# Storing the residual gate in rows of 512 bytes, and loading a gate tile behind its unit's weights

## The chip, the cores and the metric

The kernel runs on one core of one Trainium2 chip. The metric is the device time of one execution in microseconds (us), the median of several runs. Lower is better.

## The reference: one layer of a hybrid diffusion block

256 latent tokens and 256 context tokens of width 2048 pass through one layer: a modulated norm, one wide input projection, a bidirectional recurrent branch of 16 heads (RWKV-7), a latent attention branch of 8 heads, and a merge. Only the end matters for the change:

```python
sh_x, sc_x, g_x = modulation(c, w_mod[i], b_mod[i])      # g_x: the residual gate, 2048 values
...
def merge_branches(o_rwkv, o_mla, gate_logits, w_br_r, w_br_m, w_out):
    g_r, g_m = jnp.split(jax.nn.sigmoid(gate_logits), 2, axis=-1)
    return (g_r * (o_rwkv @ w_br_r) + g_m * (o_mla @ w_br_m)) @ w_out
...
x_new = x + g_x * merge_branches(o_rw_x, o_ml_x, mg_x, w_branch_rwkv[i], w_branch_mla[i], w_out[i])
```

So there are two kinds of gates: the *merge gates* (`gate_logits`, 2 x 2048 values for each token) and the *residual gate* `g_x` (one value for each of the 2048 columns).

## The kernel before: how the work is staged

**Matmuls.** Every large matmul is done in three passes for accuracy. A weight piece `w` of 128 x 512 float32 is loaded by SP's DMA queue (L236, in `piece`), ScalarE (ACT) casts it to a high part `wh`, VectorE (DVE) subtracts to get a low part `wl` (both in `parts_of`, through helpers whose line is L141), and TensorE (PE) runs high x high, high x low and low x high (L114, L116, L119). A *half* of a unit is one weight piece: four blocks of 128 by 128, thus 12 matmuls. `weights` issues the loads of both pieces of a unit first, and then hands them out one by one:

```python
247  def weights(src, n, pool=None, ns=None):
249      ws = [piece(src[:, n // 2 * i:n // 2 * i + n // 2], [P, n // 2], pool) for i in range(2)]
250      for w in ws:
251          yield parts_of(w, pool, ns)
```

**Buffers.** Up to a switch late in the kernel, the pool `wp` holds 4 buffers for `w`, 3 for `wh`, 2 for `wl`. After the switch (`place[:] = mg, NWL, NSX, NSX`, L1437) units use the pool `mg`, with 8, 4 and 4. The gate tiles `th` have 2 buffers in `wp` and 4 in `mg`.

**Order.** A scheduler sets one static order for each engine, from priorities and from a planner's estimate; the casts and subtractions of weights (`HP`) get priority. At run time each engine, and SP with its DMA issues too, goes through its own list strictly in order. An instruction whose semaphores are not there holds up everything behind it on the same engine.

**Stages.** The norm and the first projection come first. The recurrent branch follows, with further projections running between its steps as background work (the units of `bg_z`, `merge_gate_g` and others). Then comes attention, whose background ends with the first merge branch. The second merge branch (`w_br[1]`) and the output projection (`w_out`) end the kernel.

**The residual gate.** 32 small products with `w_mod_g` run as background in the recurrent stage and are summed into `gT`, 128 partitions x 16 columns: the value of gate column 128 c + p stands at partition p, column c. It goes to a DRAM tile `gd` of 16 x 128 (L1450), and is read back four times for the output projection, each time as four rows repeated for all partitions (`gx`, L1472). The store of L1450 writes through a transposed view, so each run in memory is one float32 of 4 bytes. In the program it stands behind the attention, but it waits for nothing but `gT`, and the scheduler puts it into the recurrent stage.

**The merge's first branch.** `merge_gate_g` has left tanh of each merge gate in the DRAM tile `thd`. `branch_g(j)`, j = 0 to 15, is one unit of background work: it loads the gate tile `th` (L1400), multiplies two halves of `w_br[0, j]`, forms (th + 1) x product on DVE, in place in `th`, and stores it back to `thd` (L1409), from where the second branch reads it (`gth`, L1456):

```python
1397 def branch_g(j):
1399     th = logits()
1400     nc.sync.dma_start(th, thd[j])
1401     ps = pp.tile([P, 512], F32, name="acc", tag="acc", bufs=2)
1402     for i, (wh, wl) in enumerate(weights(w_br[0, j], 1024)):
...
1408     V.scalar_tensor_tensor(th, th, 1.0, ps[:, 0:T], ALU.add, ALU.mult)
1409     nc.sync.dma_start(thd[j], th)
```

Units 0 to 11 take their `th` from `wp`, so a load there waits until the store two units earlier has landed and left its buffer. Units 12 to 15 take it from `mg`. The product goes to one of two `acc` buffers, so the matmuls of unit j + 2 wait for DVE's step of unit j. In the order listings below a unit is known by its numbers: before, `th_14902` with `acc_14904` is unit 7, `th_14953` unit 8, `th_15117` unit 12, and the weights are `w_14997`, `w_14999` (unit 9), `w_15038`, `w_15040` (10), `w_15079`, `w_15081` (11), `w_15120`, `w_15122` (12) and `w_15161`, `w_15163` (13). In the changed kernel the weights' numbers are lower by 2, and `th` is numbered after its weights (`th_14911` is unit 7, `th_14962` unit 8, `th_15126` unit 12).

Of the kernel before, what the change touches and what calls it, by code (L numbers as in the profile page):

```python
# [9 lines left out]
F32 = mybir.dt.float32  # L10
# [6 lines left out]
P = 128  # L17
D = 2048
KT = D // P
# [126 lines left out]
def hybrid_block(  # L146
# [20 lines left out]
    nc = tc.nc  # L167
    clock = Clock()
    V, S = Elementwise(nc.vector, clock, 960, 0.066), Elementwise(nc.scalar, clock, 1200, 0.08)
    E = Tensor(nc.tensor, clock)  # L170
# [12 lines left out]
    def con(name):  # L183
        o, w = CO[name]
        return cc[:, o:o + w]
# [5 lines left out]
    ident = con("ident")  # L191
# [41 lines left out]
    def piece(src, shape, pool=None):  # L233

        w = (pool or place[0]).tile(shape, F32, name="w", tag="w", bufs=NWU if pool else place[1])
        nc.sync.dma_start(w, src)  # L236
        return w

    def parts_of(w, pool=None, ns=None):

        h = (pool or place[0]).tile(list(w.shape), F32R, name="wh", tag="wh", bufs=ns or place[2])
        l = (pool or place[0]).tile(list(w.shape), F32R, name="wl", tag="wl", bufs=ns or place[3])
        with tc.high_priority(HP):
            split(w, h, l)
        return h, l

    def weights(src, n, pool=None, ns=None):

        ws = [piece(src[:, n // 2 * i:n // 2 * i + n // 2], [P, n // 2], pool) for i in range(2)]
        for w in ws:  # L250
            yield parts_of(w, pool, ns)

    def mm3(ps, ah, al, bh, bl, start, stop):

        E.matmul(ps, lhsT=ah, rhs=bh, start=start, stop=False)
        E.matmul(ps, lhsT=ah, rhs=bl, start=False, stop=False)
        E.matmul(ps, lhsT=al, rhs=bh, start=False, stop=stop)
# [16 lines left out]
    pp = ctx.enter_context(tc.tile_pool(name="pp", bufs=2, space=PSUM))  # L274
# [157 lines left out]
    gT = cst.tile([P, KT], F32, name="gT")  # L432
# [33 lines left out]
    thd = dr1.tile([2 * KT, P, T], F32, name="thd")  # L466
# [688 lines left out]
    with tc.tile_pool(name="ml", bufs=2) as ml:  # L1155
# [238 lines left out]
        def logits():  # L1394
            return wp.tile([P, T], F32, name="th", tag="th", bufs=2)

        def branch_g(j):

            th = logits()
            nc.sync.dma_start(th, thd[j])  # L1400
            ps = pp.tile([P, 512], F32, name="acc", tag="acc", bufs=2)
            for i, (wh, wl) in enumerate(weights(w_br[0, j], 1024)):
                with E.burst(tc):
                    for k in range(4):
                        cs = slice(128 * k, 128 * k + 128)
                        mm3(ps[:, 0:T], wh[:, cs], wl[:, cs], *(t[:, 4 * i + k] for t in ob[0]), i + k == 0, i * 4 + k == 7)
                yield
            V.scalar_tensor_tensor(th, th, 1.0, ps[:, 0:T], ALU.add, ALU.mult)
            nc.sync.dma_start(thd[j], th)  # L1409

        brought = False
        for j in range(KT):
            main.append(((lambda j=j: brought and len(extra) == 0), branch_g(j)))
# [15 lines left out]
    mg = ctx.enter_context(tc.tile_pool(name="mg", bufs=2))  # L1429
# [14 lines left out]
    while gate_left:  # L1444
        ps = pp.tile([P, 512], F32, name="acc", tag="acc", bufs=2)
# [1 line left out]
    if gsum:  # L1447
        gate_sum()
    gd = dr1.tile([KT, P], F32, name="gd")
    nc.sync.dma_start(gd.rearrange("c p -> p c"), gT)  # L1450
    mh = mg.tile([P, KT, T], F32R, name="mh", bufs=1)
    ml_ = mg.tile([P, KT, T], F32R, name="mlo", bufs=1)
    for j in range(KT):
        th = [mg.tile([P, T], F32, name=f"gth{b}") for b in range(2)]
        for b in range(2):
            nc.sync.dma_start(th[b], thd[16 * b + j])  # L1456
        ps = pp.tile([P, 512], F32, name="chp", tag="ch", bufs=2)
# [149 lines left out]
```

## Time and profile before

| What | Value |
|---|---|
| time, median of 3 runs | 1277.62 us (1274.62 to 1279.53) |
| the profiled execution: its own time, and its span | 1277.28 us, 1275.5 us |
| PE busy | 1211.3 us, 95% of the span |
| DVE busy, ACT busy | 953.0 us (75%), 577.1 us (45%) |
| DMA | 212.10 MB, mean 166 GB/s; 68560 of 172320 packets under 512 B |
| mean granted PE clock | 0.992 |

PE = TensorE, PEld = its weight loads, DVE = VectorE, ACT = ScalarE, SPq = SyncE's DMA issues. Times within the profile count from the start of the span. In a row of the timeline, the figure in brackets is how long the engine stood idle before the instruction, and what ended that. A stretch of the windows view gives busy us for each engine, then the granted clock (1.00 is full speed), the share of time in which the DMA engines were busy, and GB/s.

### The profile page before, as it was taken

The page shows a single profiled execution, that of the slowest core. Times are in us where ns is not written, and L with a number is a line of the kernel's source. Part 1 is how long each engine was busy: PE and PEld are TensorE (multiplying, and loading weights), DVE is VectorE, ACT ScalarE, POOL GpSimd, SP SyncE. Part 2 cuts the span into 40 slices and gives each one's busy share as a digit, 9 for nine tenths or more (in the row PEclk, how much of TensorE's full clock was granted, in tenths as well). Part 3 has the DMA queues.
Part 4 walks back from the last instruction along what each step waited for, and adds up shares of the span by engine and source line. Part 5 has one row for each costly group of instructions (what it writes and reads, how often), then busy time and mean ns, then how long its engine had stood idle before and what let it go on. Part 6 is the DMA issues. An engine that isn't in the chain of part 4 may idle for free. (4 is left out here: it accounts for less than half of the span.)

```text
span 1275.5 us, 30066 instructions
## 1 busy us (share of the span) xinstructions
PE 1211.3 (95%) x11484; PEld 1027.0 (81%) x11484; DVE 953.0 (75%) x2658; ACT 577.1 (45%) x1215; POOL 3.3 (0%) x9
## 2 busy tenths in 40 slices
PE   5999999999999989999999997999999999899998
PEld 2566878778887877887788787989899999899887
DVE  4444777877898878888978886875876777769655
ACT  3444543442444424524434343444565555535443
POOL 0000000000000000000000000000000000000000
PEclk9999999998999999999999998999999999999999
DMA  9998445443442434533434354434765433589684
GB/s 375 355 365 313 134 143 166 145 127 103 132 121 84 137 80 112 141 111 102 140 92 146 83 148 118 114 81 148 229 212 167 123 118 109 182 274 295 225 259 140
DMA packets 172320, 212.10 MB, mean 166 GB/s; under 512 B 68560, under 2 KB 96848, under 8 KB 171664
## 3 DMA queue, kind: packets, MB, share of 16 engines
q1 hardware_dynamic: 172176, 210.18, 52.9%
q8 instruction: 90, 1.47, 0.5%
q14 instruction: 54, 0.44, 0.1%
HBM read 195.30 MB, written 14.82 MB: 165 GB/s over the span
## 5 line engine op out<-in xcount | busy, mean ns | idle before, releaser
L141 ACT CAST wh<-w 128x512 fp32r<-128x512 f32 (+1 forms) x484 | 290.9, 607 | 359.4 <-PE acc L119 139.4
L141 DVE TENSOR_TENSOR wl<-w,wh 128x512 fp32r<-128x512 f32 (+1 forms) x480 | 322.4, 674 | 145.2 <-ACT wh L141 70.6
L119 PE MATMUL acc<-hmh,wl 128*128 128x256 f32 (+1 forms) x1312 | 398.3, 304 | 5.3 <-DVE wl L141 4.9
L119 PE MATMUL acc<-hml,wh 128*128 128x256 f32 (+1 forms) x1312 | 394.9, 301 | 0.0
L119 PE MATMUL acc<-hmh,wh 128*128 128x256 f32 (+1 forms) x928 | 274.2, 296 | 0.0
L119 PEld LDWEIGHTS acc<-hmh,wl 128*128 128x128 f32 x1312 | 249.2, 190 | 20.7 <-DVE wl L141 9.2
L119 PEld LDWEIGHTS acc<-hml,wh 128*128 128x128 f32 x1312 | 250.0, 191 | 9.3 <-issue 1.0
L119 PEld LDWEIGHTS acc<-hmh,wh 128*128 128x128 f32 x928 | 176.8, 190 | 4.9
L116 PE MATMUL acc<-hmh,wh 128*128 128x256 f32 (+1 forms) x384 | 145.2, 378 | 13.1 <-ACT wh L141 8.6
L116 PEld LDWEIGHTS acc<-hmh,wh 128*128 128x128 f32 x384 | 72.8, 190 | 38.9 <-ACT wh L141 14.8
L141 DVE TENSOR_TENSOR pr<-wt 64x14 f32<-64x14 f32 (+6 forms) x224 | 42.6, 190 | 3.4
L141 DVE TENSOR_TENSOR wt<-wt,pr 64x14 f32<-64x14 f32 (+6 forms) x224 | 42.3, 189 | 3.3
L114 PE MATMUL a<-hmh,wh 128*128 128x512 f32 x96 | 40.7, 424 | 0.0
L141 DVE TENSOR_TENSOR W<-WT,lv 128x512 f32<-128x512 f32 x48 | 32.2, 683 | 8.7 <-PE lv L114 8.7
L114 PE MATMUL pm<-wm,ssil 128*32 128x256 f32 x512 | 34.5, 385 | 4.5 <-DMA wm<-in_w_mod_ss 4.4
L114 PE MATMUL a<-hmh,wl 128*128 128x512 f32 x96 | 38.0, 395 | 0.4 <-DVE wl L141 0.4
L114 PE MATMUL a<-hml,wh 128*128 128x512 f32 x96 | 37.9, 395 | 0.0
L114 PE MATMUL lv<-W,Z 64*64 64x64 f32 x1024 | 33.8, 220 | 3.9 <-DVE W L141 3.9
L114 PEld LDWEIGHTS lv<-W,Z 64*64 64x64 f32 x1024 | 31.7, 135 | 5.9 <-DVE W L141 5.1
L114 PE MATMUL chp<-obh,wh 128*128 128x256 f32 x128 | 36.2, 283 | 0.0
L114 PE MATMUL chp<-obl,wh 128*128 128x256 f32 x128 | 36.2, 283 | 0.0
L114 PE MATMUL chp<-obh,wl 128*128 128x256 f32 x128 | 36.2, 283 | 0.0
(324 smaller groups left out, 2164.6 us busy)
## 6 DMA issues: line engine op xcount, KB each, us to landing
w<-in_w_proj SPq DMA_DIRECT2D x296, 256.0 KB, 3.0
wm<-in_w_mod_ss SPq DMA_DIRECT2D x64, 512.0 KB, 7.3
w<-in_w_mod_g SPq DMA_DIRECT2D x64, 256.0 KB, 3.1
w<-in_w_br SPq DMA_DIRECT2D x64, 256.0 KB, 4.1
w<-in_w_out SPq DMA_DIRECT2D x64, 256.0 KB, 3.5
w<-in_w_first SPq DMA_DIRECT2D x32, 192.0 KB, 4.9
thd<-th SPq DMA_DIRECT2D x48, 128.0 KB, 3.1
xT<-in_xcT SPq DMA_DIRECT2D x4, 1024.0 KB, 9.0
```

The costliest lines, as they stand in the source:

```text
L114: return self.engine.matmul(out, lhsT=lhsT, rhs=rhs, **kw)
L116: self.head.append(self.engine.matmul(out, lhsT=lhsT, rhs=rhs, **kw))
L119: i = self.engine.matmul(out, lhsT=lhsT, rhs=rhs, **kw)
L141: return fn(out, *a, **kw)
```

## The change

Two edits. In `branch_g` the tile `th` is made, and its load issued, inside the loop when the first half arrives: behind both weight loads of the unit instead of ahead of them. And `gT` is transposed on PE into a PSUM tile of 16 x 128, copied by ACT to a new tile `gr`, and stored to `gd` from there, as 16 rows of 512 bytes.

```diff
         def branch_g(j):
-            th = logits()
-            nc.sync.dma_start(th, thd[j])
             ps = pp.tile([P, 512], F32, name="acc", tag="acc", bufs=2)
             for i, (wh, wl) in enumerate(weights(w_br[0, j], 1024)):
+                if not i:
+                    th = logits()
+                    nc.sync.dma_start(th, thd[j])
                 with E.burst(tc):
...
     gd = dr1.tile([KT, P], F32, name="gd")
-    nc.sync.dma_start(gd.rearrange("c p -> p c"), gT)
+    ps = pp.tile([P, 512], F32, name="wk", tag="wk", bufs=2)
+    E.transpose(ps[0:KT, 0:P], gT, ident)
+    gr = mg.tile([KT, P], F32, name="gr", bufs=1)
+    S.copy(gr, ps[0:KT, 0:P])
+    nc.sync.dma_start(gd, gr)
```

In SP's list, in the recurrent stage: a weight piece, the gate's store, two weight pieces, a store of the recurrent output. First before, then after.

```order
L236 DMA w_10417<-in_w_proj 128x512
L1450 DMA gd_15281<-gT_1344 128x16x1
L236 DMA w_10466<-in_w_proj 128x512
L236 DMA w_10468<-in_w_proj 128x512
L1076 DMA orwd_1354<-y_10087 128x256
```

```order
L236 DMA w_10417<-in_w_proj 128x512
L236 DMA w_10466<-in_w_proj 128x512
L236 DMA w_10468<-in_w_proj 128x512
L1076 DMA orwd_1354<-y_10087 128x256
L236 DMA w_10512<-in_w_proj 128x512
```

The gate's store has left this place, and the weight pieces follow each other. The engines' lists stand otherwise as before up to the first merge branch.

In SP's list in the first merge branch, from the store of unit 6 on, before and then after:

```order
L1409 DMA thd_1348<-th_14840 128x256
L236 DMA w_15038<-in_w_br 128x512
L1400 DMA th_15117<-thd_1348 128x256
L1400 DMA th_14953<-thd_1348 128x256
L236 DMA w_15120<-in_w_br 128x512
L236 DMA w_15040<-in_w_br 128x512
L236 DMA w_15122<-in_w_br 128x512
L236 DMA w_15079<-in_w_br 128x512
```

```order
L1410 DMA thd_1348<-th_14849 128x256
L236 DMA w_15036<-in_w_br 128x512
L236 DMA w_15118<-in_w_br 128x512
L1403 DMA th_14962<-thd_1348 128x256
L236 DMA w_15120<-in_w_br 128x512
L236 DMA w_15038<-in_w_br 128x512
L1403 DMA th_15126<-thd_1348 128x256
L236 DMA w_15077<-in_w_br 128x512
```

Unit 12's first weight piece has moved ahead of unit 8's gate load, and unit 12's gate load behind both of its pieces. Unit 12's second piece still follows unit 8's gate load. Units 0 to 11 had their gate loads behind their own weights already: the scheduler had put those loads, which wait for a buffer, there.

DVE's list at the same place (`obl` is the low part of attention's output), before and then after:

```order
L141 TENSOR_TENSOR wl_15018<-w_14999,wh_15017 128x512
L141 TENSOR_TENSOR wl_15125<-w_15120,wh_15124 128x512
L141 SCALAR_TENSOR_TENSOR th_14902<-th_14902,acc_14904 128x256
L141 TENSOR_TENSOR wl_15141<-w_15122,wh_15140 128x512
L141 SCALAR_TENSOR_TENSOR th_14953<-th_14953,acc_14955 128x256
L141 TENSOR_TENSOR wl_15043<-w_15038,wh_15042 128x512
L141 TENSOR_TENSOR wl_15166<-w_15161,wh_15165 128x512
```

```order
L141 TENSOR_TENSOR wl_15018<-w_14997,wh_15017 128x512
L141 TENSOR_TENSOR wl_15123<-w_15118,wh_15122 128x512
L141 TENSOR_TENSOR wl_15141<-w_15120,wh_15140 128x512
L141 SCALAR_TENSOR_TENSOR th_14911<-th_14911,acc_14902 128x256
L141 SCALAR_TENSOR_TENSOR th_14962<-th_14962,acc_14953 128x256
L141 TENSOR_TENSOR wl_15164<-w_15159,wh_15163 128x512
L141 TENSOR_TENSOR wl_15182<-w_15161,wh_15181 128x512
```

DVE's step of unit 7 now stands behind both of unit 12's subtractions instead of one, and that of unit 8 follows it at once.

The store of the gate is now here, in SP's list between the store of unit 10 and the loads of the second branch:

```order
L1410 DMA thd_1348<-th_15003 128x256
L1403 DMA th_15249<-thd_1348 128x256
L1410 DMA thd_1348<-th_15044 128x256
L1455 DMA gd_15281<-gr_15284 16x128
L1461 DMA gth0_15289<-thd_1348 128x256
L1403 DMA th_15085<-thd_1348 128x256
```

It waits for ACT's copy `gr`. PE's transpose stands between units 8 and 9, and ACT's copy right behind the cast of unit 12's second piece.

## Prediction

> **What bounds the kernel.** The page comes first: PE is busy for 95% of the span and leads the chain that ended last. What can be won is PE's idle time and its slow time.
>
> ```profile
> PE 1211.3 (95%) x11484; PEld 1027.0 (81%) x11484; DVE 953.0 (75%) x2658; ACT 577.1 (45%) x1215; POOL 3.3 (0%) x9
> PE 33%; DMA 4%; DVE 1%; ACT 1%; issue 0%; SPq 0%; DVEq 0%; ACTq 0%
> ```
>
> DMA's part of that chain is small, so the question is where it sits. The list of DMA issues (count, KB each, median us to landing):
>
> ```profile
> w<-in_w_proj SPq DMA_DIRECT2D x296, 256.0 KB, 3.0
> dl<-AQ SPq DMA_DIRECT2D x128, 8.0 KB, 1.5
> gd<-gT SPq DMA_DIRECT2D x1, 8.0 KB, 12.2
> ```
>
> The gate's store moves 8 KB in 12.2 us. `dl` moves 8 KB in runs of 64 bytes and lands in 1.5 us; the gate's runs have 4 bytes, so there are 2048 of them. Weight pieces (time to landing, min/median/max) from 500 to 700 us and from 765 to 800 us:
>
> ```profile
> DMA to landing us min/median/max: 2.4/3.0/5.5
> ```
>
> ```profile
> DMA to landing us min/median/max: 2.5/3.2/13.2
> ```
>
> One piece beside the gate's store took 13.2 us. SP's timeline, then the chain of waits, name it:
>
> ```profile
> 777.00 0.45 SPq L1450 DMA_DIRECT2D gd<-gT  x1
> 777.67 2.88 SPq L236 DMA_DIRECT2D w<-in_w_proj  x2
> ```
>
> ```profile
> 777.67 13.20 DMA w<-in_w_proj
> ...
> 790.97 0.62 ACT wh L141
> 791.58 0.29 ACT th L141
> ```
>
> The piece issued right behind the gate's store lands at 790.87. ACT's cast `wh` waits for it, and the activation `th` stands behind that cast. PE's timeline and two windows (PE, PEld, DVE, ACT, POOL busy; clock; DMA share; GB/s) show the damage:
>
> ```profile
> 784.85 0.60 PE L126 MATMUL wk<-cc,BK 128*128 128x128 f32 x4
> 791.64 0.58 PE L116 MATMUL acc<-hmh,wh 128*128 128x256 f32 x1 [6.19 <-ACT wh L141]
> 792.98 0.58 PE L119 MATMUL acc<-hmh,wl 128*128 128x256 f32 x1 [0.54 <-DVE wl L141]
> 797.64 0.60 PE L126 MATMUL wk<-cc,BK 128*128 128x128 f32 x4
> 797.99 0.36 PE L116 MATMUL acc<-hmh,wh 128*128 128x256 f32 x1
> ```
>
> ```profile
> 792.00:794.00 2.00, 1.46 (x7) 1.16 (x6) 1.93 (x6) 1.58 (x3) 0.00 (x0) 0.50 0.16 43
> 794.00:796.00 2.00, 2.00 (x11) 2.00 (x11) 1.71 (x8) 0.62 (x1) 0.00 (x0) 0.50 0.67 222
> ```
>
> PE stands idle for 6.19 us, and then runs at a granted clock of 0.50.
>
> **Part 1, the gate's store.** What leaves this place is the 4-byte store. The pieces behind it keep their order, and with the usual 3.0 us the first of them would land at about 780.7, before ACT wants it. The price has three readings.
>
> The lowest is the idle time alone, 6.2 us. The highest counts PE alone. From the transposes at 784.85 to those at 797.64 PE did two halves in 12.79 us. At full clock a half takes 1.40 us, by these two pieces of the chain (each is 11 of a half's 12 matmuls):
>
> ```profile
> 1129.35 1.29 PE acc L119 x11
> 1130.75 1.29 PE acc L119 x11
> ```
>
> Four transposes take 0.35 us (797.64 to 797.99). So 3.15 us would do, and 9.6 us come back.
>
> The third asks what is late next, and that is DVE with ACT. DVE, ACT and PE, in this order:
>
> ```profile
> 791.90 0.42 DVE L141 SCALAR_TENSOR_TENSOR gz<-th,acc 128x256 f32<-128x256 f32 x1 [7.81 <-ACT th L141]
> 797.89 0.69 DVE L141 TENSOR_TENSOR wl<-w,wh 128x512 fp32r<-128x512 f32 x1 [0.81 <-PE acc L119]
> 803.54 1.28 DVE L141 TENSOR_TENSOR_SCAN En<-restart,En 128x260 f32<-128x260 f32 x2
> ```
>
> ```profile
> 799.77 0.66 ACT L141 COPY wt<-wt 64x256 f32<-64x256 f32 x1 [0.67 <-DVE wt L141]
> ```
>
> ```profile
> 806.06 0.39 PE L119 MATMUL acc<-hmh,wl 128*128 128x256 f32 x1 [0.15 <-DVE wl L141]
> ```
>
> DVE's `gz` needs the finished unit, whose matmuls end just ahead of the transposes (about 785.0), and ACT's `th`, some 0.4 us: it can start at about 785.5, not 791.90, so 6.4 us earlier. From there DVE works nearly without a gap; only its wait of 0.81 us for PE at 797.89 drops out, as PE is then further ahead. That makes 7.2 us. ACT's copy `wt` waits for DVE, the activations behind it feed DVE's scan at 803.54, and PE waits at 806.06 for a `wl` that stands behind that scan. So PE's lead beyond DVE's is given back there, all but some 0.1 us. I take **7.3 us**, since PE is seen to wait for DVE there, and keep 6.2 and 9.6 as ends.
>
> What the edit adds: one PE transpose (0.15 us, a quarter of the 0.60 at 797.64) and one small ACT copy (under the 0.62 us of a cast). Both stand in the branch, where PE is about to wait 3.23 us and ACT waits for weights (next part), so they cost nothing; without that cover, under 0.8 us. The new store has 16 runs of 512 bytes. By its bytes and its fewer runs it should land like `dl`, in 1.5 us, at most like a weight piece in 3.0. It is issued some 16 us ahead of its first reader:
>
> ```profile
> L1472 SPq DMA_DIRECT2D gx<-gd x4: 422/422/469, 1139.3 to 1234.7; - x4
> ```
>
> On SP it waits for ACT's copy, done long before; behind it stand the second branch's loads.
>
> **Part 2, the gate loads in the first branch.** PE waits here twice (PE's timeline, then the chain of waits):
>
> ```profile
> 1114.54 0.35 PE L116 MATMUL acc<-hmh,wh 128*128 128x256 f32 x1 [3.23 <-DVE th L141]
> 1128.96 0.38 PE L116 MATMUL acc<-hmh,wh 128*128 128x256 f32 x1 [1.12 <-DVE th L141]
> ```
>
> ```profile
> 1105.86 3.36 DMA thd<-th
> 1109.61 3.09 DMA w<-in_w_br
> 1113.37 0.69 DVE wl L141
> 1114.06 0.34 DVE th L141
> 1121.87 3.92 DMA thd<-th
> 1125.81 2.59 DMA th<-thd
> ```
>
> First wait: the store of unit 6 lands at 1109.22. SP's gate load of unit 8 waits for it, and with it all behind, so unit 12's pieces go out from 1109.61. The first lands after 3.09 us, is cast and split, and only then comes DVE's step of unit 7, for which unit 9's matmuls wait. Now one of the two pieces of unit 12 goes ahead of that gate load, but the other is still behind it, out at 1109.6 as before, and DVE's step of unit 7 now stands behind the `wl` of *both*. So that step comes at about 1114.0 again. Unit 8's step follows at once, earlier than before, but nobody waits for it.
>
> Second wait: store of unit 9, 3.92 us, load of unit 11 into the same buffer, 2.59 us, DVE's step of unit 11, for which unit 13 waits. These two transfers, and DVE's order ahead of them, stay. I take **0** for this part. Its ends: a gain of 3.23 + 1.12 us and the slow clock behind the first wait (about 1.5 us, from the window below), 5.9 in all; a loss of 3.8 us (the third rival).
>
> ```profile
> 1115.00:1120.00 5.00, 5.00 (x32) 5.00 (x31) 3.01 (x5) 2.71 (x5) 0.00 (x0) 0.68 0.85 287
> ```
>
> Sum: 7.3 + 0. The profiled execution took 1277.28 us, 0.3 under the median of 1277.62; less 7.3 us it is **1270.0 us**.
>
> **The rivals.**
>
> *PE keeps its whole lead.* 8.6 to 9.6 us come back, 1268 us. For it speaks that half of the loss is slow clock, which the two windows show at 0.50; against it PE's wait for DVE at 806.06. [...] 12 in 100.
>
> *The branch's waits go too.* If unit 12's earlier piece lets DVE pass sooner, up to 5.9 us come on top: 1264 us. Against it stands the order on DVE. 8 in 100.
>
> *The branch gets worse; the one that can end slower.* DVE's step of unit 7 depends on one more weight piece. Landing times of pieces from 1100 to 1140 us:
>
> ```profile
> DMA to landing us min/median/max: 2.9/4.2/5.2
> ```
>
> At 5.2 instead of 3.09 us PE waits 2.1 us longer, and an idle time of over 5 us may cost a slow stretch like that after 6.19 us, twice as long as the one here: 1.7 us more. That is 3.8 us, 1273.8 us. It ends slower than before if the piece takes longer than about 8.7 us. 8 in 100, with 4 for the slower end.
>
> *The store was not the cause.* The late piece and the store only coincide, and 1277 us remain. Against it: of some 300 pieces that one alone took so long. 5 in 100.
>
> *Only part comes back.* Another load or DVE is late again within 10 us, and 3 to 6 us remain as the gain: about 1273 us. 17 in 100.
>
> **How the numbers follow.** The forecast case (6.2 to 8.6 us) has 50 in 100. The runs shown spread by 4.9 us, so 0.5%, or 6.4 us, is about what can be told from no change. Faster by more than that are most of the forecast case and the first two rivals: 0.66. Within it: the part gain, the absent cause, most of the worse branch, the rim of the forecast: 0.30. Slower: 0.04. The range of 1265 to 1275 us reaches from the branch's gain almost to the worse branch with a bad median, and leaves out the ends of both.
>
> **What would show it.** Right: no weight piece over 6 us around 780, no wait of PE over 1.5 us from 784 to 800, clock 1.00 there; the gate's store landing in under 3 us at about 1117; PE's two waits in the branch about 7 us earlier and as long as before. Wrong: another wait of some us between 785 and 815, or a branch whose PE idle time differs from 4.4 us by more than 1.5.

## The result and the profile after

The changed kernel takes 1267.43 us in the median of 4 runs (1267.39 to 1267.55). The kernel before took 1278.41 us on the same chip (1274.62 to 1279.53). The ratio on record is 0.9923, with a 95% interval of 0.9898 to 0.9947 (the two medians alone give 0.9914). The profiled execution took 1267.55 us, with a span of 1265.7 us.

The page of the changed kernel, its lines on busy time and on the chain that ended last:

```profile
span 1265.7 us, 30073 instructions
PE 1208.8 (96%) x11485; PEld 1023.7 (81%) x11485; DVE 953.7 (75%) x2658; ACT 577.6 (46%) x1216; POOL 3.3 (0%) x9
PE 33%; DMA 3%; DVE 2%; issue 1%; ACT 1%; SPq 0%; DVEq 0%; ACTq 0%
```

PE works 2.5 us less than before and stands idle some 7 us less. DMA's part of the chain fell from 4% to 3%. To see where the time came back, take the start of one and the same matmul in both traces and subtract. The difference is the lead of the changed kernel; it is worked out from the two traces, not a view of the profile.

```
start before, us    763.1   791.6   816.6   841.8  1092.8  1142.9  1268.5
lead, us            -0.18    6.24    8.73    8.95    9.22    9.77    9.77
```

So 9.13 us come back between 763 and 842 us, 0.27 between there and the branch, and 0.55 in the merge's first branch. In the rest of the text, the *gain* of a kernel in a stage is the growth of its lead over the profiled run of the kernel before: in the *recurrent place* from 763 to 842 us, in the *branch* from 1093 to 1143 us.

**The recurrent place.** SP's timeline after: the gate's store no longer stands among the weight pieces, and the first three go out as one group.

```profile
776.25 4.51 SPq L236 DMA_DIRECT2D w<-in_w_proj  x3
781.91 8.35 SPq L236 DMA_DIRECT2D w<-in_w_proj  x6
```

Weight pieces from 765 to 800 us, time from issue to landing. The largest was 13.2 us before:

```profile
DMA to landing us min/median/max: 2.6/3.0/3.8
```

PE's timeline after, at the two groups of transposes that had the stall between them, then at the first wait behind:

```profile
785.04 0.60 PE L126 MATMUL wk<-cc,BK 128*128 128x128 f32 x4
788.28 0.60 PE L126 MATMUL wk<-cc,BK 128*128 128x128 f32 x4
797.33 0.39 PE L119 MATMUL acc<-hmh,wl 128*128 128x256 f32 x1 [0.77 <-DVE wl L141]
```

The way between the two groups takes 3.24 us, where it took 12.79. The windows (PE, PEld, DVE, ACT, POOL busy; clock; DMA share; GB/s) show full clock and work on PE in nearly all of these twenty microseconds. Before, by windows of 1 us, the clock stood at 0.50 from about 790.5 to 797.4 us.

```profile
780.00:790.00 10.00, 9.86 (x82) 9.50 (x81) 9.49 (x34) 5.77 (x12) 0.00 (x0) 1.00 0.52 158
790.00:800.00 10.00, 9.23 (x118) 8.49 (x118) 8.99 (x20) 6.93 (x16) 0.00 (x0) 1.00 0.43 112
```

DVE's timeline after, at the two steps that the prediction named:

```profile
784.31 0.42 DVE L141 SCALAR_TENSOR_TENSOR gz<-th,acc 128x256 f32<-128x256 f32 x1
794.80 1.29 DVE L141 TENSOR_TENSOR_SCAN En<-restart,En 128x260 f32<-128x260 f32 x2 [0.53 <-ACT En L141]
```

`gz` starts 7.59 us earlier than at 791.90, the scan 8.74 us earlier than at 803.54, and PE's next wait stands 8.73 us earlier than at 806.06. One matmul ahead of that wait PE's lead was still 9.36 us (805.63 before, 796.27 after).

**The branch.** PE's waits after, and the two windows of 15 us around them:

```profile
1105.58 0.55 PE L116 MATMUL acc<-hmh,wh 128*128 128x256 f32 x1 [3.37 <-DVE th L141]
1119.19 0.39 PE L116 MATMUL acc<-hmh,wh 128*128 128x256 f32 x1 [0.49 <-DVE th L141]
```

```profile
1100.00:1115.00 15.00, 11.63 (x86) 11.36 (x85) 10.22 (x17) 6.44 (x11) 0.00 (x0) 0.89 0.87 286
1115.00:1130.00 15.00, 14.51 (x124) 14.31 (x124) 7.60 (x14) 5.59 (x9) 0.00 (x0) 1.00 0.84 269
```

Both waits are still there, 9.0 and 9.8 us earlier than before. DVE's step of unit 7 and that of unit 8 now run as one group of two, as the order said:

```profile
1105.02 0.74 DVE L141 SCALAR_TENSOR_TENSOR th<-th,acc 128x256 f32<-128x256 f32 x2
```

The gate's new store is issued at 1114.52 us and lands after 3.6 us:

```profile
1114.52 0.43 SPq L1455 DMA_DIRECT2D gd<-gr  x1
```

### The profile page after: what moved, and what is told of

It is laid out like the page before. It is cut to its first block, busy times and chain, and to the rows that moved or that the text cites. A ratio compares the mean times of both kernels' runs of the same rounds, so it can differ in the third digit from the quotient of the medians.

```text
span 1265.7 us, 30073 instructions
## 1 busy us (share of the span) xinstructions
PE 1208.8 (96%) x11485; PEld 1023.7 (81%) x11485; DVE 953.7 (75%) x2658; ACT 577.6 (46%) x1216; POOL 3.3 (0%) x9
```

## The experiments

The theory at the start: the 4-byte form of the store makes a weight piece late, PE stalls for it, and DVE with ACT limit what comes back; the order of the gate loads is worth nothing. Rivals: the branch edit has a share in the gain; the store's *place* is at fault, not its form; SP's queue is at fault, and another queue would do. A later rival is about what in the form is slow.

| kernel | median, us | ratio to before (95% interval) | gain at the recurrent place, us | gain in the branch, us |
|---|---|---|---|---|
| changed kernel | 1267.43 | 0.9923 (0.9898 to 0.9947) | 9.13 | 0.55 |
| store edit alone | 1268.91 | 0.9914 (0.9891 to 0.9936) | 8.74 | 0.45 |
| branch edit alone | 1277.76 | 0.9995 (0.9976 to 1.0014) | -0.01 | -0.81 |
| rows of 512 bytes, stored early | 1269.08 | 0.9923 (0.9901 to 0.9946) | 8.56 | -1.36 |
| 4-byte runs, stored late | 1283.35 | 1.0033 (1.0019 to 1.0046) | 8.98 | -10.95 |
| half of the 4-byte runs | 1276.62 | 0.9986 (0.9964 to 1.0007) | 4.70 | -0.36 |
| the 4-byte store twice | 1285.73 | 1.0050 (1.0030 to 1.0071) | -6.04 | 0.40 |
| the 4-byte store on ACT's queue | 1277.56 | 0.9997 (0.9973 to 1.0021) | 2.32 | -1.22 |
| gate loads on GpSimd's queue | 1277.38 | 0.9995 (0.9979 to 1.0011) | 9.81 | -7.51 |
| scratch: 4 bytes, 64 apart | 1266.91 | 0.9918 (0.9890 to 0.9947) | 8.37 | -1.03 |
| scratch: 4 bytes, 512 apart | 1269.68 | 0.9935 (0.9912 to 0.9957) | 8.54 | 0.71 |
| scratch: 128 runs of 4 bytes | 1273.90 | 0.9969 (0.9951 to 0.9987) | 6.50 | 0.38 |
| scratch: 128 runs of 64 bytes | 1269.76 | 0.9936 (0.9912 to 0.9961) | 8.85 | 0.02 |

The kernel before had medians of 1278.82, 1278.51 and 1279.3 us in the three groups of runs. Single runs of one kernel mostly lie within some 3 us of its median, a few up to 9 us off. Part of that arises ahead of 763 us, where the leads of these kernels differ by 8.5 us though their programs do the same work up to there. So the gains by stage say more of a mechanism than the medians do.

### Each edit alone

The store edit alone is the second part of the diff on the kernel before, the branch edit alone the first part.

> The kernel before with the gate's store alone changed (PE transpose, ACT copy, 16 rows of 512 bytes); gate loads of the first branch as before. Theory A (the 2048 runs of 4 bytes held up the weight pieces queued behind them, and nearly all of the gain is that): about 9 us under before, some 1268 us; no weight piece over 6 us near 780; the branch's PE waits stay at 3.2 and 1.1 us. Rival B (the branch's gate loads made the gain): within 2 us of before. Rival C (both needed): a gain of 4 to 6 us.

> The kernel before with the order of the gate loads in the first branch alone changed; the 4-byte store stays at 777 us. Theory A: within 1 us of before (the changed kernel's two PE waits in the branch were 3.37 and 0.49 us against 3.23 and 1.12), PE still idle some 6 us near 785. Rival B: 8 to 10 us under before. Rival C: 4 to 6 us under before.

With the store edit alone the gain at the recurrent place is 8.74 us, no piece there takes over 4.0 us, and the ratio is that of the whole change. With the branch edit alone the old stall is there as it was; PE's timeline of that kernel:

```profile
795.43 0.58 PE L116 MATMUL acc<-hmh,wh 128*128 128x256 f32 x1 [5.66 <-ACT wh L141]
796.77 0.58 PE L119 MATMUL acc<-hmh,wl 128*128 128x256 f32 x1 [0.55 <-DVE wl L141]
1119.78 0.38 PE L116 MATMUL acc<-hmh,wh 128*128 128x256 f32 x1 [4.06 <-DVE th L141]
```

In the branch PE waits 4.06 and 1.23 us there, 3.60 and 0.33 us with the store edit alone, 3.37 and 0.49 with both, 3.23 and 1.12 with neither. The gains in the branch, with the edit and without it, lie between -1.4 and +0.7 us in no order (but for the two kernels below whose edit acts in the branch). So the gain is the store's, and the order of the gate loads is worth 0 within about 1 us.

### Is it the form of the store, or its place?

The first kernel is the changed one with the transpose, copy and store moved into the recurrent stage, where `gT` is complete. The second is the changed one with ACT's copy, but without the transpose: the 4-byte runs are stored at the late place.

```diff
 early512
     def gate_sum():
...
+        if b == 7:
+            ps = pp.tile([P, 512], F32, name="wk", tag="wk", bufs=2)
+            nc.tensor.transpose(ps[0:KT, 0:P], gT, ident)
+            gr = rw.tile([KT, P], F32, name="gr")
+            nc.scalar.copy(gr, ps[0:KT, 0:P])
+            nc.sync.dma_start(gd, gr)
...
```

```diff
 late4
-    ps = pp.tile([P, 512], F32, name="wk", tag="wk", bufs=2)
-    E.transpose(ps[0:KT, 0:P], gT, ident)
-    gr = mg.tile([KT, P], F32, name="gr", bufs=1)
-    S.copy(gr, ps[0:KT, 0:P])
-    nc.sync.dma_start(gd, gr)
+    gr = mg.tile([P, KT], F32, name="gr", bufs=1)
+    S.copy(gr, gT)
+    nc.sync.dma_start(gd.rearrange("c p -> p c"), gr)
```

> The changed kernel, but transpose, copy and the store of 16 rows of 512 bytes are issued in the recurrent stage, as soon as the last gate column is there, at nearly the place of the old 4-byte store. Theory A (the form of the runs): as the changed kernel, 1267 to 1269 us, and no weight piece behind it over 6 us. Rival D (the place: any store there holds up the pieces behind it): 1275 to 1278 us, with PE idle some 6 us near 785.

> The changed kernel, but ACT copies the gate without a transpose and the store stays one of 2048 runs of 4 bytes, at the changed kernel's place in SP's list in the first branch. Theory A (the form): the loads behind it come some 10 us late: the gate load of unit 11, for which PE waits at once, and the second branch's; PE idle 6 to 10 us near 1120, 1274 to 1279 us in all. Rival D (the place): 1267 to 1269 us.

In rows of 512 bytes the store does no harm at the early place: it is issued at 766.0 us, lands in 1.4 us, and the gain is 8.56 us. In 4-byte runs it does its harm at the late place. From SP's timeline, the chain of waits and PE's timeline of that kernel:

```profile
1115.67 0.43 SPq L1453 DMA_DIRECT2D gd<-gr  x1
1117.26 0.38 SPq L1403 DMA_DIRECT2D th<-thd  x1
```

```profile
1117.26 11.13 DMA th<-thd
```

```profile
1128.94 0.58 PE L116 MATMUL acc<-hmh,wh 128*128 128x256 f32 x1 [9.10 <-DVE th L141]
```

A gate load issued 1.6 us behind the store takes 11.13 us, and PE waits 9.10 us for it; the gain of the recurrent place is lost again. The time of 1283.35 us lies above the range expected for the form (1274 to 1279): the branch loses 10.95 us, more than the wait itself, and 2.4 us more go behind it. It is the form, at either place.

### How much of it, and on which queue?

Three kernels go out from the kernel before. One stores columns 8 to 15 as before (1024 runs) and the other half in rows at the late place. One stores all of `gT` a second time, right behind the first, into a scratch tensor (4096 runs in all). One issues the same old store from ACT:

```diff
 half4
-    nc.sync.dma_start(gd.rearrange("c p -> p c"), gT)
+    nc.sync.dma_start(gd[8:16].rearrange("c p -> p c"), gT[:, 8:16])
+    ps = pp.tile([P, 512], F32, name="wk", tag="wk", bufs=2)
+    E.transpose(ps[0:8, 0:P], gT[:, 0:8], ident)
+    gr = mg.tile([8, P], F32, name="gr", bufs=1)
+    S.copy(gr, ps[0:8, 0:P])
+    nc.sync.dma_start(gd[0:8], gr)
```

```diff
 double4
     nc.sync.dma_start(gd.rearrange("c p -> p c"), gT)
+    gd2 = dr1.tile([KT, P], F32, name="gd2")
+    nc.sync.dma_start(gd2.rearrange("c p -> p c"), gT)
```

```diff
 act4
-    nc.sync.dma_start(gd.rearrange("c p -> p c"), gT)
+    nc.scalar.dma_start(gd.rearrange("c p -> p c"), gT)
```

> The kernel before, but only columns 8 to 15 of the gate are stored in runs of 4 bytes (1024 runs) at the old place; columns 0 to 7 go through a PE transpose and 8 rows of 512 bytes in the first branch. Theory A (time in proportion to the runs, about 5 us per 1024): the weight piece behind lands after 7 to 8 us instead of 13.2, PE idle near 785 falls from 6.2 to about 1 us, 1268 to 1271 us. Rival (a fixed price of any 4-byte store): the piece still takes about 13 us, 1276 to 1279 us.

> The kernel before with the 4-byte store issued twice in a row, the second time to a scratch tile: 4096 runs. Theory A (proportion): the piece behind lands after 23 to 25 us, PE idle near 785 is 15 to 17 us, some 10 us over before, 1288 us. Rival (a fixed price): as before.

> The kernel before with the 4-byte store issued on ACT's DMA queue instead of SP's, at nearly the same time. Theory E (the 16 DMA engines are shared, whatever queue the store stands in): the weight piece beside it is as late as before or half as late, 7 to 13 us, 1272 to 1279 us. Theory F (only what stands behind it in the same queue waits): weight pieces on SP's queue land in 3 to 4 us, PE idle near 785 under 1 us, 1267 to 1270 us, though the store itself still takes over 10 us.

More of it costs more: the stores land after 9.9 us (1024 runs), 12.2 us (2048), and 15.5 and 17.8 us (twice 2048), and the gain at the recurrent place goes 4.70, 0, -6.04 us. The two expectations of a price in proportion fail, though, and so do their rivals of a fixed price. With 1024 runs the piece behind landed after 9.6 us, neither 7 to 8 nor 13 (the median of 1276.62 us alone would fit the fixed price, the gain of 4.70 us does not). With 4096 it landed after 17.6 us, not 23 to 25. With two stores PE's wait grows from 6.19 us to this:

```profile
801.14 0.58 PE L116 MATMUL acc<-hmh,wh 128*128 128x256 f32 x1 [12.64 <-ACT wh L141]
```

So this is no price per run alone: a line through the three points would leave about 7 us for no runs at all. That gap led to the last group of kernels.

ACT's queue does not help. The store goes out at 767.73 us, almost 9 us earlier in the work, and lands after 11.42 us (chain of waits of that kernel). Now the eight loads of `dl` that SP issues beside it, from 767.7 to 773.0 us, are late. Their landing, in that kernel and then in the kernel before:

```profile
767.73 11.42 DMA gd<-gT
```

```profile
DMA to landing us min/median/max: 5.3/9.6/10.5
```

```profile
DMA to landing us min/median/max: 1.5/1.5/1.6
```

SP itself then stands from 773.3 to 779.2 us, and PE waits 4.72 us at 782.68. The weight pieces that SP issues only after that land within 4.6 us: what came late was not the piece that theory E named, but the loads of `dl`, and SP behind them. So a store on ACT's queue made loads on SP's queue late, 9.6 us in the median instead of 1.5: theory F, by which only the store's own queue waits, falls. Theory E's reason, shared DMA engines, no run here shows by itself. Why a weight load of SP waited 5.9 us for that store's landing, as the profile has it, stays open too.

### Gate loads on another queue

The rest of the branch's waits seemed to hang on SP being held up by gate loads. The changed kernel with these loads issued by GpSimd:

```diff
 th_pool
-                    nc.sync.dma_start(th, thd[j])
+                    nc.gpsimd.dma_start(th, thd[j])
```

> The changed kernel with the gate loads of the first branch on GpSimd's DMA queue, so that SP's weight pieces no longer stand behind a load that waits for a store. If SP's order is what makes PE wait 3.4 us there: unit 12's second piece goes out some 2 us earlier, that wait falls under 1.5 us, the slow clock behind it goes, 1263 to 1266 us. If DMA traffic or DVE's order sets the wait whatever the queue, or GpSimd's issue is slow: 1267 us or more.

It loses 7.51 us in the branch and another 2.2 us between the recurrent place and the branch, and with that nearly all of the change's gain. SP's timeline, then the chain of waits, then PE's timeline of that kernel:

```profile
1102.80 7.11 SPq L236 DMA_DIRECT2D w<-in_w_br  x11
```

```profile
1105.35 6.05 DMA w<-in_w_br
...
1124.17 5.74 DMA th<-thd
```

```profile
1113.24 0.55 PE L116 MATMUL acc<-hmh,wh 128*128 128x256 f32 x1 [6.17 <-DVE th L141]
1130.57 0.39 PE L116 MATMUL acc<-hmh,wh 128*128 128x256 f32 x1 [2.84 <-DVE th L141]
```

The first wait grew from 3.37 to 6.17 us, but the queue is not all that changed: the scheduler gave DVE another order too. DVE's timeline from its last `obl` up to the steps of units 7 and 8, in the changed kernel, then in this one:

```profile
1102.88 1.29 DVE L141 TENSOR_TENSOR wl<-w,wh 128x512 fp32r<-128x512 f32 x2
1104.41 0.69 DVE L141 TENSOR_TENSOR wl<-w,wh 128x512 fp32r<-128x512 f32 x1 [0.25 <-ACT wh L141]
1105.02 0.74 DVE L141 SCALAR_TENSOR_TENSOR th<-th,acc 128x256 f32<-128x256 f32 x2
```

```profile
1107.74 2.12 DVE L141 TENSOR_TENSOR wl<-w,wh 128x512 fp32r<-128x512 f32 x3
1110.38 0.69 DVE L141 TENSOR_TENSOR wl<-w,wh 128x512 fp32r<-128x512 f32 x1 [0.52 <-ACT wh L141]
1112.07 0.69 DVE L141 TENSOR_TENSOR wl<-w,wh 128x512 fp32r<-128x512 f32 x1 [1.00 <-ACT wh L141]
1112.68 0.74 DVE L141 SCALAR_TENSOR_TENSOR th<-th,acc 128x256 f32<-128x256 f32 x2
```

The step of unit 7 stands behind three subtractions in the changed kernel and behind five here. The third is through at 1109.86 us and the step starts at 1112.68; these 2.82 us are as much as the wait grew by. The last of the five waits for a weight piece that took 6.05 us. So this wait is the second case of the expectation, DVE's order. PE's later wait of 2.84 us hangs on unit 11's gate load, which took 5.74 us, against 3.11 us in the changed kernel's chain. SP issues 11 weight pieces in one go here, and pieces from 1100 to 1130 us land after 4.8 us in the median (4.1 in the changed kernel). Whether their traffic or GpSimd's queue made that gate load late is not shown. Nor does this kernel tell what a free SP alone would be worth, because DVE's order changed with the queue.

### What in the form is slow: many runs, short runs, or runs side by side?

Four kernels are the changed one plus one more store of `gT` at the old place, into a scratch tensor that nobody reads. They differ in the layout of the scratch tensor and in the number and length of the runs; the lists of SP, DVE and ACT are otherwise those of the changed kernel near this place:

```diff
 spread64 (2048 runs of 4 bytes, each 64 bytes from the next)
+    pr = dr1.tile([KT, P, 16], F32, name="pr")
+    nc.sync.dma_start(pr[:, :, 0:1].rearrange("c p o -> p c o"), gT.unsqueeze(2))
 spread512 (the same, 512 bytes apart)
+    pr = dr1.tile([KT, P, P], F32, name="pr")
+    nc.sync.dma_start(pr[:, :, 0:1].rearrange("c p o -> p c o"), gT.unsqueeze(2))
 few4 (one column: 128 runs of 4 bytes, side by side)
+    pr = dr1.tile([KT, P], F32, name="pr")
+    nc.sync.dma_start(pr[0:1].rearrange("c p -> p c"), gT[:, 15:16])
 run64 (128 runs of 64 bytes)
+    pr = dr1.tile([P, KT], F32, name="pr")
+    nc.sync.dma_start(pr, gT)
```

> The changed kernel, with a second store of the gate put back at the old place: again 2048 runs of 4 bytes, but each run 64 bytes from the next, in a scratch tensor that nobody reads. Theory 'number of runs': the price is one per run, wherever it lands. The scratch store takes 11 to 13 us to land as the old one did (12.2 us), the weight piece behind it over 9 us, TensorE waits 5 to 7 us near 785, and the time is within 3 us of the kernel before. Rival 'neighbours': it is the writes of 4 bytes into one short stretch of memory that wait for each other (in the old store 128 runs lie side by side in each row of 512 bytes). Then the scratch store lands in under 5 us, no piece from 765 to 800 us takes over 6 us, TensorE does not wait there, and the time is that of the changed kernel, near 1268 us.

> The same with each run of 4 bytes 512 bytes from the next. Theory 'number of runs': as above, 11 to 13 us, TensorE waits 5 to 7 us, within 3 us of the kernel before. Rival 'neighbours': under 5 us and near 1268 us; if 64 bytes apart is still slow and 512 apart fast, the stretch in which runs hinder each other is longer than 64 bytes.

> The changed kernel, with only the last of the 16 gate columns stored a second time at the old place: 128 runs of 4 bytes, side by side in 512 bytes of a scratch tensor. By the line through the stores of 1024, 2048 and 4096 runs (9.9, 12.2 and 17.8 us; some 2.3 to 2.8 us for each 1024 runs on top of about 7) it would land after 7 us even with few runs. Theory 'number of runs': most of that 7 us is no price of the runs, so 128 runs land in 1.5 to 3 us, no weight piece takes over 5 us, the time is near 1268 us. Rival 'neighbours': 128 runs in one stretch of 512 bytes wait for each other as those of each row of the old store did, all rows at once; it lands in 7 us or more, the weight piece behind it is late by some us, and TensorE waits 1 to 3 us near 785; near 1272 us.

> The changed kernel, with all 8 KB of the gate stored a second time at the old place, not turned: 128 runs of 64 bytes, one for each partition, in a scratch tensor. Both theories: few runs, each a line of its own or nearly, land like the 8 KB loads of runs of 64 bytes (1.5 us), at most 4 us; no weight piece over 6 us, no wait of TensorE near 785, near 1268 us. A third view, that every run under 512 bytes is slow, has it land in over 6 us with a late weight piece.

Landing of the scratch store in these four kernels, in the same order:

```profile
DMA to landing us min/median/max: 5.5/5.5/5.5
```

```profile
DMA to landing us min/median/max: 5.4/5.4/5.4
```

```profile
DMA to landing us min/median/max: 8.4/8.4/8.4
```

```profile
DMA to landing us min/median/max: 3.1/3.1/3.1
```

2048 runs of 4 bytes that do not lie side by side land in 5.5 us, a little over the 5 us expected of this rival, and cost PE almost nothing. 128 runs that do lie side by side land in 8.4 us, sixteen times fewer runs and yet slower, and PE waits for the late piece. PE's timeline from 780 to 792 us, first with 2048 runs 64 bytes apart, then with 128 side by side:

```profile
784.47 0.39 PE L119 MATMUL acc<-hmh,wl 128*128 128x256 f32 x1 [0.15 <-DVE wl L141]
```

```profile
787.40 0.38 PE L116 MATMUL acc<-hmh,wh 128*128 128x256 f32 x1 [0.94 <-ACT wh L141]
788.74 0.39 PE L119 MATMUL acc<-hmh,wl 128*128 128x256 f32 x1 [0.84 <-DVE wl L141]
```

The slowest weight piece near this place took 5.8 and 6.2 us with runs 64 and 512 bytes apart (the rival had said not over 6), 7.9 with 128 side by side and 3.7 with runs of 64 bytes, against 3.8 without a scratch store. The gains at the recurrent place are 8.37 and 8.54 us (apart), 6.50 (128 side by side), 8.85 (runs of 64 bytes). The kernels with no 4-byte store here range from 8.56 to 9.81. So spread over the memory, all 2048 runs cost 0.7 us at most, hardly more than the scatter; side by side they cost 9.1. The number of runs alone is not the price: what cost time in these kernels is writes of 4 bytes next to each other, and among these more runs did take longer (8.4, 9.9 and 12.2 us for 128, 1024 and 2048). A distance of 64 bytes was enough to be rid of the stall (no wait of PE over 0.15 us from 780 to 792 us); shorter ones were not run.

What traffic does meanwhile shows in the DMA view of the window from 778 to 784 us, in 40 slices of 0.15 us, first of the kernel before, then of the one with runs 64 bytes apart:

```profile
GB/s 150 259 341 232 289 183 37 24 65 8 6 2 0 1 1 0 0 0 0 0 0 0 0 0 0 0 0 0 0 0 0 0 0 0 41 41 0 150 177 82
DMA packets 2226, 0.31 MB, mean 52 GB/s; under 512 B 2080, under 2 KB 2080, under 8 KB 2225
```

```profile
GB/s 341 287 96 116 41 123 177 205 273 219 248 183 103 104 77 8 6 3 2 2 1 0 0 0 0 55 82 150 191 150 191 273 178 137 137 177 307 389 375 266
DMA packets 2592, 0.85 MB, mean 142 GB/s; under 512 B 2118, under 2 KB 2249, under 8 KB 2591
```

In both the small packets are through by about 781 us. With runs apart the loads are back from 781.7 us on. With runs side by side nothing moves until 783.1 us, and by windows of 1 us no more than 31 GB/s from 784 to 789 us. The third view of the last expectation falls: runs of 64 bytes landed in 3.1 us. Nor does the length of a run alone sort these stores: 2048 runs of 4 bytes apart took 5.5 us, 128 of 4 bytes side by side 8.4. That writes next to each other wait for each other, the rival's reading, fits these times, but no run here shows the cause itself.

## Why the prediction was right, and which term was off

**What stalls PE, and what ends it: right.** No weight piece takes over 3.8 us near 780 us (foretold: none over 6), PE does not wait by more than 0.77 us from 784 to 800 us (foretold: none over 1.5), the clock from 780 to 800 us is 1.00. The store edit alone gives 8.74 of the 9.13 us, so the rival "the store was not the cause" falls. The reason given for the slow store, its number of runs, was only half a reason: 2048 runs that lie apart landed in 5.5 us, 128 side by side in 8.4.

**The term of 7.3 us was mis-sized; it measured 9.1.** The mechanism stands: DVE with ACT limits what comes back, and PE gives its lead beyond DVE's back at the named wait, which grew from 0.15 to 0.77 us. The step that failed is the start of `gz`. The prediction put the end of its unit just ahead of the transposes, at about 785.0 us, and so `gz` at 785.5. In the trace after, with the same work on PE up to there, the activation `th` runs at 783.25 and `gz` at 784.31 us; the half that PE does between the unit's end and the transposes was overlooked. The prediction's own row for `gz` had the size: DVE stood idle for 7.81 us ahead of it. Counted with the 0.18 us by which the changed kernel was late there, `gz` gained 7.8 us instead of 6.4. Between `gz` and the scan another 1.15 us came back instead of 0.81, and 0.2 us behind PE's wait. Less the 0.1 us that the prediction had added there, these are the 1.8 us that were missing. So the size is that of the rival "PE keeps its whole lead" (8.6 to 9.6 us, 1268 us), the limit that of the forecast: it took back 0.63 us of PE's lead (9.36 to 8.73). That rival's remark that half of the loss is slow clock counts too much: of 9.6 us, 6.7 are idle time (6.19 and 0.54) and some 2.9 slow clock. With the idle time gone, the slow stretch of 0.50 is gone too, and in the branch an idle time of 3.37 us is still followed by a slow one (0.89 in the window from 1100 to 1115 us). Before, PE worked at 0.50 from 791.6 to about 797.4 us until the full clock was back; what sets the length of such a stretch, no run here shows.

**The branch at 0: right within the scatter.** The two waits stayed (3.86 us together, 4.35 before; 0.55 us by the lead). The kernel without this edit gained 0.45 us there, the one with this edit alone lost 0.81, so the 0.55 us cannot be put down to it. The reason given holds too: DVE's step of unit 7 stands behind both subtractions of unit 12, and unit 8's came with it.

**What the edit adds: right, but for one number.** The transpose (0.27 us, right ahead of PE's wait of 3.37 us) and the copy (0.25 us, within it) cost nothing that shows. The new store took 3.6 us where the prediction said under 3; nobody waited for it.

**The forecast time** of 1270.0 us is 2.6 above the median: 1.8 us of it are the term's, and the 0.55 us of the branch and the 0.27 ahead of it lie within the scatter.

## What to carry to other kernels

Look in the list of DMA issues for small stores that land late, and then at the load issued right behind: here the price was paid by that load (13.20 us to landing) and by PE, which stood 6.19 us for it. Scalars of 4 bytes that are written next to each other to memory from many partitions were the costly case (12.2 us for 2048, 8.4 us for 128). One transpose and a copy turned them into rows (1.4 and 3.6 us) and ended the stall. A spacing of 64 bytes (5.5 us) ended it too, in a scratch tensor that nobody reads back. The other place and the other queue that were tried did not: PE still waited 9.10 and 4.72 us. When a stall goes, the gain is found by following the second engine's own chain, from the last instruction that the stalled engine had really finished ahead of the stall.

## What was not expected of the hardware

- 128 writes of 4 bytes side by side (512 bytes) landed in 8.4 us, 2048 of them spread by 64 bytes in 5.5 us, and 16 runs of 512 bytes in 1.4 and 3.6 us.
- Such a store held up transfers of another queue: loads of 8 KB issued by SP took 9.6 us in the median instead of 1.5 while the store ran on ACT's queue.
- One and the same work takes differently long from run to run: up to 763 us the traces lie up to 8.5 us apart. No run here shows why.
